# Starting the second DMA queue of an ifftshift copy three steps further on

## The chip, the cores and the metric

The kernel runs on one core of a Trainium2 chip. The metric is the device time of one execution in microseconds, lower is better. A difference between two kernels is judged from the medians of their runs.

## The reference

The kernel computes an inverse FFT shift of a square float32 matrix. For an even size this exchanges the quadrants: the upper half of the rows changes place with the lower half, and the left half of the columns with the right half.

```python
x = np.random.randn(8192, 8192).astype(np.float32)
out = np.fft.ifftshift(x)      # out[r, c] = x[(r + 4096) % 8192, (c + 4096) % 8192]
```

Nothing is calculated. Each of the 8192 rows is 32 KiB long and is copied in two halves of 16 KiB, 268.44 MB in all, and the same amount is read and written.

## The kernel before, in words

The copy goes from HBM to HBM by DMA. No tile in on-chip memory is used, and no compute engine takes part, apart from four small memsets that the framework puts at the start.

The rows of the output are taken in steps of 16 (`ENGINES`, line 9), one row for each of the core's 16 DMA engines. One DMA covers 32 steps (`per`, line 25), so 512 rows, and one half of the columns. Its access pattern (line 26) has three dimensions: 16 rows next to each other, then 32 steps of 16 rows, then 4096 elements in a piece. The first dimension is the one that is spread over the DMA engines. Each engine thus gets 32 packets of 16 KiB from one DMA, for rows that are 16 apart, and a last small packet that updates the semaphore of that DMA.

The loop over `row` (line 27) makes 16 rounds. In each round two DMAs are issued (lines 29 and 30): the left half of the output (`h = 0`) on the SP queue, and the right half (`h = hc`) on the scalar queue. In the profile the SP queue is q1 and the scalar queue q10 (its issues are shown under ACTq). The left half of an output row is read from the right half of the source row, and the other way round. The source row is half the matrix away: `src_row = (row + hr) % R`, 4096 rows or 128 MiB.

Both queues feed the same 16 DMA engines. No DMA depends on the data of another. The framework gives every DMA one of eight semaphores in turn, four to each queue, so an issue waits until the DMA four places before it on the same queue has landed. The order of the packets on an engine is set by the order of the DMAs on each queue and by how the engine takes turns between the two queues.

Of the kernel before, what the change touches and what calls it, by code (L numbers as in the profile page):

```python
# [1 line left out]

# [4 lines left out]


ENGINES = 16


@with_exitstack
def kernel(
    ctx: ExitStack,
    tc: tile.TileContext,
    x: bass.AP,
    out: bass.AP,
):
    nc = tc.nc
    R, C = x.shape  # L20
    hr = R // 2
    hc = C // 2


    per = 32
    dims = [[C, ENGINES], [ENGINES * C, per], [1, hc]]
    for row in range(0, R, ENGINES * per):
        src_row = (row + hr) % R
        for queue, h in ((nc.sync, 0), (nc.scalar, hc)):
            queue.dma_start(  # L30
                out=bass.AP(out.tensor, out.offset + row * C + h, dims),
                in_=bass.AP(x.tensor, x.offset + src_row * C + hc - h, dims),
            )


# [1 line left out]
_INS = ['x']  # L37
_OUTS = [((8192, 8192), 'float32')]


def kernel(**inputs):
    import numpy as _np
    import concourse.bacc as _bacc
    import concourse.tile as _tile
    from concourse import mybir as _mybir
    from concourse.bass_utils import run_bass_kernel_spmd as _run

    nc = _bacc.Bacc("TRN2", target_bir_lowering=False, num_devices=1)  # L48
    arrays, args = {}, []
    for name in _INS:  # L50
        a = _np.ascontiguousarray(inputs[name])
        if a.dtype.kind in "iu":
            a = a.astype(_np.int64)
        arrays[f"in_{name}_dram"] = a
        args.append(nc.dram_tensor(f"in_{name}_dram", a.shape, _mybir.dt.from_np(a.dtype), kind="ExternalInput").ap())
    for i, (shape, dtype) in enumerate(_OUTS):
        dt = _mybir.dt.from_np(_np.dtype(dtype))
        args.append(nc.dram_tensor(f"out_{i}_dram", shape, dt, kind="ExternalOutput").ap())
    with _tile.TileContext(nc) as tc:
        kernel(tc, *args)  # L60
    r = _run(nc, [arrays], core_ids=[0])
    got = tuple(r.results[0][f"out_{i}_dram"] for i in range(len(_OUTS)))
    return got[0]
```

## Time and profile before

| what | value |
|---|---|
| median of 3 runs | 821.4 us (821.02 to 823.58) |
| the profiled execution | 822.98 us, its span 821.2 us |
| DMA packets | 16896, 268.44 MB, mean 327 GB/s |
| HBM read and written together | 654 GB/s over the span |
| share of the 16 engines' span, SP queue (q1) | 50.2% |
| share of the 16 engines' span, scalar queue (q10) | 49.0% |
| DMA issues | 16 on each queue, 8192 KB each, about 204 us from issue to landing |

The span runs from the first to the last instruction of the program. The share of a queue is the time that its packets took, as a part of 16 engines' span; both shares together say how full the DMA engines are. The two rows of forty figures in the prediction cut the span into 40 equal slices, 20.5 us each: the first row is the busy share of the DMA engines in tenths (9 is 90% or more), the second is what they moved in GB/s. A DMA view can also be asked for a short stretch of the span. It then gives, for each queue, the number of packets that start in it, the MB they moved and the share. A line of issues gives the number of instructions and the KB of each. A line of the timeline gives start and duration in microseconds. An issue's duration includes the time in which it waits for room in the queue.

### The profile page before, as it was taken

The numbers are of one execution on the slowest core, as the hardware profiler recorded it, in microseconds if no ns is written. First come the engines' busy times: TensorE is split into PE (matmuls) and PEld (weight loads), VectorE is DVE, ScalarE is ACT, GpSimd is POOL, SyncE is SP. The second block draws the span as 40 slices with busy tenths as digits, with TensorE's granted clock in tenths as the row PEclk, the third lists the DMA queues.
The fourth block names the chain that finished last, engine by engine and source line by source line (L and its number), as shares of the span: only waits on it lengthen the run. The fifth ranks groups of instructions, "written<-read, shape, count | busy, mean of one in ns | idle before, by whom it ended". The sixth has DMA issues, their size and how long they took to land. (4 is left out here: it accounts for less than half of the span.)

```text
span 821.2 us, 77 instructions
## 1 busy us (share of the span) xinstructions
POOL 0.2 (0%) x4
## 2 busy tenths in 40 slices
POOL 0000000000000000000000000000000000000000
DMA  8999999999999999999999999999999999999998
GB/s 296 333 324 329 331 328 334 330 330 329 327 330 329 331 326 332 332 327 328 330 330 330 330 323 330 324 330 330 332 326 329 330 322 333 329 329 327 330 329 276
DMA packets 16896, 268.44 MB, mean 327 GB/s; under 512 B 512, under 2 KB 512, under 8 KB 512
## 3 DMA queue, kind: packets, MB, share of 16 engines
q1 hardware_dynamic: 8448, 134.22, 50.2%
q10 hardware_dynamic: 8448, 134.22, 49.0%
HBM read 268.44 MB, written 268.44 MB: 654 GB/s over the span
## 5 line engine op out<-in xcount | busy, mean ns | idle before, releaser
L48 POOL MEMSET const-bfloat16-1.0<- 128x1 bf16 x1 | 0.1, 102 | 0.0
L48 POOL MEMSET const-uint8-127<- 128x1 uint8 x1 | 0.1, 102 | 0.0
L48 POOL MEMSET const-float32-0.0<- 128x1 f32 x1 | 0.1, 99 | 0.2 <-issue 0.2
L48 POOL MEMSET const-float32-1.0<- 128x1 f32 x1 | 0.1, 99 | 0.0
## 6 DMA issues: line engine op xcount, KB each, us to landing
out_dram<-in_x_dram ACTq DMA_DIRECT2D x16, 8192.0 KB, 204.1
out_dram<-in_x_dram SPq DMA_DIRECT2D x16, 8192.0 KB, 204.0
```

The source lines that it names most:

```text
L48: nc = _bacc.Bacc("TRN2", target_bir_lowering=False, num_devices=1)
```

## The change

A step is still 16 rows. The left halves are issued as before: 16 DMAs of 32 steps on the SP queue. The right halves, on the scalar queue, begin with step 3 (`lead = 3`) and come round to steps 0 to 2 at the end. The function `pieces` cuts the steps so that no DMA crosses a multiple of 32 steps, where the source row would wrap at the middle of the matrix. The scalar queue thus has 17 DMAs: one of 29 steps, fifteen of 32 and one of 3. The issues of the two queues still alternate in the program, and bytes, packet sizes and the split over the engines stay as they are.

```diff
     per = 32
-    dims = [[C, ENGINES], [ENGINES * C, per], [1, hc]]
-    for row in range(0, R, ENGINES * per):
+    lead = 3
+    steps = R // ENGINES
+
+    def copy(queue, h, first, n):
+
+        dims = [[C, ENGINES], [ENGINES * C, n], [1, hc]]
+        row = first * ENGINES
         src_row = (row + hr) % R
-        for queue, h in ((nc.sync, 0), (nc.scalar, hc)):
-            queue.dma_start(
-                out=bass.AP(out.tensor, out.offset + row * C + h, dims),
-                in_=bass.AP(x.tensor, x.offset + src_row * C + hc - h, dims),
-            )
+        queue.dma_start(
+            out=bass.AP(out.tensor, out.offset + row * C + h, dims),
+            in_=bass.AP(x.tensor, x.offset + src_row * C + hc - h, dims),
+        )
+
+    def pieces(first, last):
+
+        while first < last:
+            n = min(per, last - first, per - first % per)
+            yield first, n
+            first += n
+
+    lefts = list(pieces(0, steps))
+    rights = list(pieces(lead, steps)) + list(pieces(0, lead))
+    for k in range(max(len(lefts), len(rights))):
+        if k < len(lefts):
+            copy(nc.sync, 0, *lefts[k])
+        if k < len(rights):
+            copy(nc.scalar, hc, *rights[k])
```

## The prediction

> **What bounds the kernel now.** I read the page from the top. No compute engine matters: the only busy one is POOL, with four memsets at the start. What counts are the DMA lines.
>
> ```profile
> span 821.2 us, 77 instructions
> POOL 0.2 (0%) x4
> DMA  8999999999999999999999999999999999999998
> GB/s 296 333 324 329 331 328 334 330 330 329 327 330 329 331 326 332 332 327 328 330 330 330 330 323 330 324 330 330 332 326 329 330 322 333 329 329 327 330 329 276
> DMA packets 16896, 268.44 MB, mean 327 GB/s; under 512 B 512, under 2 KB 512, under 8 KB 512
> q1 hardware_dynamic: 8448, 134.22, 50.2%
> q10 hardware_dynamic: 8448, 134.22, 49.0%
> HBM read 268.44 MB, written 268.44 MB: 654 GB/s over the span
> out_dram<-in_x_dram ACTq DMA_DIRECT2D x16, 8192.0 KB, 204.1
> out_dram<-in_x_dram SPq DMA_DIRECT2D x16, 8192.0 KB, 204.0
> ```
>
> The reader is to see that the 16 DMA engines are busy from the third microsecond to the last few, at an even 322 to 334 GB/s between the two end slices. The time is therefore the number of packets on one engine times the mean time of a packet, and a change can help only through that mean, the head or the tail. Of the 8448 packets of a queue, 256 are semaphore updates (16 DMAs on 16 engines) and 8192 move 16 KB. From the shares, a data packet took 0.502 x 16 x 821.2 / 8192 = 805 ns on q1 (SP) and 0.490 x 16 x 821.2 / 8192 = 786 ns on q10 (scalar). An engine moves 512 of each: 412.2 + 402.4 = 814.6 us. The first packet starts at 2.1 us, so the engines end near 816.7 on average; some 4.5 us of the 821.2 are then the spread of the engines and the closing. The profiled execution took 822.98 us, 1.8 more than its span and 1.6 above the median of 821.4.
>
> The second thing to read is how the queues stand to each other. I asked the DMA view for the stretch from 2 to 4.9 us and for one from 815.1 to 818 us:
>
> ```profile
> q1 hardware_dynamic: 60, 0.98, 98.1%
> ...
> q10 hardware_dynamic: 59, 0.82, 81.1%
> q1 hardware_dynamic: 19, 0.08, 8.2%
> ```
>
> In the first stretch only q1 runs: 60 packets, nearly four per engine, before q10 sends anything. At the end it is turned round: q10 moves 0.82 MB while q1 has 0.08 MB left. The issues late in the run show the same distance, since each waits for the landing of the DMA four places before it on its queue:
>
> ```profile
> 614.16 39.30 SPq L30 DMA_DIRECT2D out_dram<-in_x_dram  x1
> 618.85 39.97 ACTq L30 DMA_DIRECT2D out_dram<-in_x_dram  x1
> ```
>
> That is 4.69 us, and a pair of packets takes 805 + 786 = 1591 ns, so the distance is 2.95, that is three steps. I also followed single engines through the packet records (the next packet starts 3 to 4 ns before the recorded end of the one before). Nearly every engine starts q1, q1, q1, q1, q10, and then alternates; between q1's semaphore update and q10's lie three data packets of each queue, all through the run. So an engine now copies the left half of step k+3, then the right half of step k, then the left of k+4, and so on: the two places are 48 rows of 32 KiB, 1.5 MiB, apart.
>
> **The change part by part.**
>
> *Order of the rights.* The scalar queue starts at step 3 and ends with steps 0 to 2. With q1 still four packets ahead at the start, an engine copies left 3, right 3, left 4, right 4: one whole row, half after half. Packets and bytes stay the same: 1024 data packets of 16 KB per engine. What can move is the mean of a packet, and no row of this trace has the two halves together. Bounds from both sides, from rows:
>
> - Gain. The fewest places at once that the trace shows is one queue alone. At the start (3.2 to 4.9 us) 44 packets of q1 took 1.033 x 16 x 1.7 / 44 = 639 ns; this is the first moment after idle. At the end (815.1 to 818 us) q10 moved 0.82 MB, 50 data packets, in 0.811 x 16 x 2.9 = 37.6 us: 752 ns. Against the mean of 795.5 in the whole run the latter is 43 ns less; for 1024 packets that is 44 us, and 160 us by the former.
> - Loss. The slowest stretch of several microseconds that I saw in the middle, 400 to 404 us, ran at 315 GB/s against 328 in 400 to 500 us. A whole run like that would be 4.1% longer, 34 us.
>
> ```profile
> q1 hardware_dynamic: 44, 0.72, 103.3%
> ...
> q1 hardware_dynamic: 1036, 16.45, 50.9%
> q10 hardware_dynamic: 1030, 16.35, 48.7%
> ```
>
> (3.2 to 4.9 us, then 400 to 500 us.) Between these ends I take the one difference the trace shows between packets that run in the same mix: q10's packets are 805 - 786 = 19 ns shorter than q1's. I assume that the second packet of a row, following its other half, gains as much again. This is a choice of size, not a measurement. It is nearer to the middle of the run than the head and tail rows, which are short and lie where engines start or fall idle. 512 x 19 ns = 9.7 us off.
>
> Why a gain at all: four address streams (left read, left write, right read, right write) in two stretches of rows for x and two for out become one stretch of x and one of out. Within a pair, the two writes of an engine cover one row of 32 KiB. If the memory pays for every new place it opens, there are fewer. That it pays for this is not shown here.
>
> *Seventeen DMAs instead of sixteen on the scalar queue* (29, fifteen times 32, and 3 steps). Each engine gets one semaphore packet more: 9 ns in the packet records, and the data packet behind one averages 26 ns above the mean of all, together 35 ns once. The extra issue is hidden: an issue that finds room takes 0.58 us (the shortest in the trace), and the one that waits does so with three DMAs of about 50 us each queued before it. It waits for its queue's thirteenth DMA, and is issued near 669 us, where its data is due at about 811 us. If that cover were gone, it would cost the issue and the time to the first packet: 0.58 + (2.1 - 0.73) = 1.9 us. Nothing on the scalar engine or SP stands behind it but the end of the kernel.
>
> *Both queues' ends of a DMA at one time.* Now q1 gives up a turn to a semaphore packet three steps before q10 does; afterwards both do so in the same round, 16 times. The trace shows no gap round such a packet, so I take 0; with 26 ns for each it is 0.4 us.
>
> *Head and tail.* SP still starts first and the scalar queue still ends with three packets per engine alone; 0 for both.
>
> A rule that speaks against the change: the Trainium skill's "DMA: Bandwidth & Descriptors", section "Latency and other measured facts", says that copies between HBM tensors fall from 214 to 103 GB/s per direction when streams in lock step are a large power of two apart (4 MiB row pitch), with channel aliasing as an unverified reason. After the change an engine's read of one half and its write of the same half, a packet apart, lie 4096 rows, 128 MiB, apart within their tensors; by that rule at full strength an estimate would be 821 x 214 / 103 = 1,707 us. Source and destination rows are 4096 apart now too, and the page shows 327 GB/s, so I keep it only as the reason of the slower rival, not as its price.
>
> *Sum.* 822.98 - 9.7 = 813.3 for the profiled execution, and 1.6 less for the median: 811.7, so 812 us.
>
> **The rivals.**
>
> 1. *The halves together help* (forecast): 812 us; its own range runs from 797 to 818.9, the lower end being half of the 44 us plus a little.
> 2. *The memory is at a fixed rate and does not care.* For it: the even rate in 38 of 40 slices, while the lefts and rights cross every position in the array, and the 1.5 MiB distance was held throughout, so nothing shows that distance matters. Time: 821.4 plus 0.4, within 0.3% (about what a measurement can tell from no change), 818.9 to 823.9.
> 3. *The change does not do what it says*: the shorter first DMA makes the scalar queue start at another distance, say two steps. Against it: the distance was set before the first DMA had ended, by the order in which the queues began, and this is not touched. A distance of one row step or so would be priced like case 2.
> 4. *Slower: the halves collide.* Now, when an engine reads the lower half of a row of x, it has just been writing the lower half of a row of out three steps on; afterwards it has just written the lower half of the corresponding row. If rows 4096 apart fall on the same parts of the memory, the read and the draining write meet there, once per pair. Price: if q10's packets lose the 19 ns by which they are shorter, 512 x 19 = 9.7 us, hence 831; at the bound 855. It decides once the mean of the packet rises by 2.4 ns (2.5 us over 1024). For it: in the packet records a third of the data packets take the shortest time, 611 ns, and one in twenty of q1 over 1.2 us, so waiting for something shared is common. Against it: each packet's own read and write are already such a pair.
>
> **How the numbers follow.** Case 1: 0.44, case 2: 0.14, case 3: 0.04, case 4: 0.38. Two signs are nearly even, because the size and the sign of the one effect are not in this trace; I lean to the gain, since fewer places at once is the one direction that the head and tail rows point to (639 and 752 ns against 795). Faster 0.44, same 0.18, slower 0.38. Eight times in ten: from 796 (half of the tail's gain and a little) to 838 (half of the loss bound), leaving about one in ten on each side. The predicted time is that of case 1.
>
> **What the profile after would show.** Right: 17 issues on the scalar queue, the first landing about 3 steps (4.8 us) earlier than now, close to SP's; later landings of both queues at nearly the same time; the same 134.22 MB per queue and one DMA more in semaphore packets (8464 on q10); q10's packets nearer 767 ns than 786, and GB/s slices near 332. Wrong: slices at 327 to 330 mean case 2; slices at 322 to 325 with q10 at 805 ns or q1 longer still mean case 4; landings of the two queues one or more steps apart mean case 3. The forecast fails if the place of the two queues in the memory does not enter the packet's time, or enters it with the other sign.

## The result

The changed kernel took 827.39 us (median of 11 runs, 826.74 to 832.63), the kernel before 822.08 us (median of 11, 819.85 to 826.24). The ratio is 1.0073, with a 95% interval of 1.0055 to 1.0092: slower by 0.7%. Here and below, a ratio and its interval are worked out from all runs of both kernels but those over 1.5% above the fastest of their own kernel, so a ratio need not equal the quotient of the two medians beside it (1.0065 here). The forecast of 812 us had the wrong sign. The range holds the time, and rival 4 (slower, 831 us) is the case that is nearest.

The page of the changed kernel. A line of the issues gives the count, the KB of each and the microseconds from issue to landing.

```profile
span 829.4 us, 78 instructions
DMA  9999999999999999999999999999999999999998
GB/s 290 329 313 318 322 315 317 326 323 335 324 320 321 328 328 326 315 333 326 330 330 317 330 333 324 329 322 335 326 333 326 330 325 332 330 332 327 330 323 273
DMA packets 16912, 268.44 MB, mean 324 GB/s; under 512 B 528, under 2 KB 528, under 8 KB 528
q10 hardware_dynamic: 8464, 134.22, 50.3%
q1 hardware_dynamic: 8448, 134.22, 48.9%
HBM read 268.44 MB, written 268.44 MB: 647 GB/s over the span
out_dram<-in_x_dram SPq DMA_DIRECT2D x16, 8192.0 KB, 205.1
out_dram<-in_x_dram ACTq DMA_DIRECT2D x15, 8192.0 KB, 205.2
out_dram<-in_x_dram ACTq DMA_DIRECT2D x1, 7424.0 KB, 54.0
out_dram<-in_x_dram ACTq DMA_DIRECT2D x1, 768.0 KB, 155.3
```

The engines are as full as before. By the same working as in the prediction, a packet of q1 now takes 0.489 x 16 x 829.4 / 8192 = 792 ns, 13 less than before, and one of q10 0.503 x 16 x 829.4 / 8192 = 815 ns, 29 more. The pair is 16 ns longer, and 512 x 16 = 8.2 us is the difference of the two spans (829.4 - 821.2). The shares are rounded; added up from the packet records, the data packets of an engine take 821.9 us instead of 814.2, 7.7 of the 8.2 us. So nearly all of the time came from the mean of a packet. (This profiled execution took 831.17 us, 3.8 above the median of its kernel.)

The order on the engines is what the change meant. The timeline late in the run shows an issue of SP and two of the scalar queue in one line (x2), start and duration. Each issue waits for the DMA four places before on its queue, and the first ones now begin 0.17 us apart, where it was 4.69 us.

```profile
622.47 38.91 SPq L34 DMA_DIRECT2D out_dram<-in_x_dram  x1
622.64 93.18 ACTq L34 DMA_DIRECT2D out_dram<-in_x_dram  x2
```

Where in the run the time went is seen when the span is cut into stretches. The columns are start and end, length, POOL's busy time, clock, DMA share and GB/s. Some stretches are left out. First the changed kernel, then the kernel before:

```profile
10.00:60.00 50.00, 0.00 (x0) 1.00 1.00 315
100.00:200.00 100.00, 0.00 (x0) 1.00 1.00 322
200.00:300.00 100.00, 0.00 (x0) 1.00 1.00 325
300.00:400.00 100.00, 0.00 (x0) 1.00 1.00 325
400.00:500.00 100.00, 0.00 (x0) 1.00 1.00 328
600.00:700.00 100.00, 0.00 (x0) 1.00 1.00 329
700.00:800.00 100.00, 0.00 (x0) 1.00 1.00 330
```

```profile
10.00:60.00 50.00, 0.00 (x0) 1.00 1.00 326
100.00:200.00 100.00, 0.00 (x0) 1.00 1.00 330
300.00:400.00 100.00, 0.00 (x0) 1.00 1.00 330
700.00:800.00 100.00, 0.00 (x0) 1.00 1.00 328
```

The changed kernel starts 3% slower and is level after about 400 us, though its order of rows is the same to the end. From the packet records, in stretches of about one DMA (51 us, the first one from 10 us on, counted from the first packet), with q1's and q10's mean packet added; the last column is the standard deviation over the 16 engines of the moment at which they reach the end of that DMA on q1:

| stretch | before, ns per pair | changed, ns per pair | before, spread us | changed, spread us |
|---|---|---|---|---|
| 1 | 1606 | 1654 | 0.40 | 0.47 |
| 2 | 1585 | 1637 | 0.49 | 0.78 |
| 4 | 1590 | 1612 | 0.74 | 0.91 |
| 8 | 1591 | 1599 | 0.79 | 0.86 |
| 12 | 1587 | 1581 | 0.79 | 0.87 |
| 16 | 1589 | 1590 | 0.77 | 1.08 |

The engines start together and drift apart, and the excess fades too. But the spread alone does not set the excess: at the end of the second stretch the changed kernel's 0.78 us is as wide as what the kernel before settles at, and in the third stretch a pair still takes 1636 ns, against 1576 before.

### The profile page after: what moved, and what is told of

The parts are those of the page before. It is cut to its first block, busy times and chain, and to the rows that moved or that the text cites. A ratio compares the mean times of both kernels' runs of the same rounds, so it can differ in the third digit from the quotient of the medians.

```text
span 829.4 us, 78 instructions
## 1 busy us (share of the span) xinstructions
POOL 0.2 (0%) x4
## 6 DMA issues: line engine op xcount, KB each, us to landing
out_dram<-in_x_dram ACTq DMA_DIRECT2D x1, 768.0 KB, 155.3
```

## The experiments

Four theories were set against each other. A: the scalar queue's read of a half of x meets the draining write of the same half of out (rival 4 of the prediction). B: the two reads in one row of x disturb each other. C: the two writes into one row of out do. D: the addresses don't matter, but both queues now end a DMA in the same round. In all runs of the first group the DMAs of both queues are cut at the same rounds, and the two offsets of the scalar queue, for reading and for writing, can be set apart (shortened, with comments added; the lines with a minus are those of the changed kernel):

```diff
-    lead = 3
+    ahead = 3          # SP's place minus the scalar queue's, in steps, at one time
+    read_lead = 3
+    write_lead = 3
-    rights = list(pieces(lead, steps)) + list(pieces(0, lead))
+    cuts = {p - ahead for p in range(per, steps, per)} | wraps   # where a source or target wraps
+    # rights: cut at cuts; lefts: cut at cuts + ahead
-            copy(nc.scalar, hc, *rights[k])
+            p, end = rights[k]
+            copy(nc.scalar, hc, (p + read_lead) % steps, (p + write_lead) % steps, end - p)
```

**Control (both 3).** The DMAs are exactly those of the changed kernel.

> Control: the changed kernel again (the scalar queue reads and writes three steps on, so both halves of a row of x and of out follow each other). All theories: about 827 us, ratio to before 1.006 to 1.009. The new profile has to show whether the excess sits in the early part of the run, as in the first profile of the changed kernel, where the two queues' packets took 1654 ns per pair in the first DMA and 1590 ns in the last (before: 1591 ns throughout); if that was a disturbance of one execution, the pairs will be equally long from start to end.

Measured: 828.63 us against 823.03, ratio 1.0043 (1.0013 to 1.0073). The new profile has the same course: 1659 ns per pair in the first stretch, 1600 in the last. The excess at the beginning belongs to the kernel and not to one execution. Three of the twelve executions took 820 to 824 us, the others 826 to 831; a possible reason stands in the last section.

**The ends of the DMAs alone.**

```diff
-    read_lead = 3
-    write_lead = 3
+    read_lead = 0
+    write_lead = 0
```

> The addresses of before (the queues 48 rows apart), but the DMAs cut so that both queues end a DMA in the same round, as in the changed kernel. If the coinciding ends cost (theory D): about 827 us, ratio 1.007. If addresses alone cost (theories A, B, C): 822 us, ratio 1.000 within 0.002.

Measured: 823.03 us against 823.03, ratio 1.0008 (0.9989 to 1.0027), and 1589 ns per pair in the first stretch. Theory D falls.

**Reads in the same rows, writes 48 rows apart.**

```diff
-    write_lead = 3
+    write_lead = 0
```

> The scalar queue reads three steps on, at the rows that SP reads, but writes where it wrote before, 48 rows behind SP; the right half of the output is thus rolled by 48 rows. Theory A (the read of a half of x meets the draining write of the same half of out): about 827 us, ratio 1.007, since the scalar queue reads the half that SP has just written. Theory B (the two reads in one row of x get in each other's way): 827 us too. Theory C (the two writes in one row of out do): 822 us. Theory D (ends of DMAs): 827 us.

Measured: 820.87 us against 823.03, ratio 0.9974 (0.9953 to 0.9995). Not slower but, if anything, a little faster: the interval ends just below 1. B falls, and A as it was put (the scalar queue reading the half that SP has just written) with it. The stretches of this run:

```profile
10.00:60.00 50.00, 0.00 (x0) 1.00 1.00 329
100.00:200.00 100.00, 0.00 (x0) 1.00 1.00 329
700.00:800.00 100.00, 0.00 (x0) 1.00 1.00 330
```

**Writes in the same rows, reads 48 rows apart.**

```diff
-    read_lead = 3
+    read_lead = 0
```

> The reverse: the scalar queue reads 48 rows behind SP, as before, but writes at the rows that SP writes; the right half of the output is rolled by 48 rows. Theory C (the two writes): about 827 us, ratio 1.007. Theories A and B (both through the read of the scalar queue): 822 us, ratio 1.000 within 0.002. Theory D: 827 us.

Measured: 850.41 us (847.35 without its two slowest runs of six) against 823.03, ratio 1.0301 (1.0264 to 1.0339). C has the sign, but the size is four times what it expected. The rate, from the fastest of the six executions, shows a loss that is deeper than in the changed kernel (313 against 322 GB/s from 100 to 200 us) and above all longer; it comes near the level of before only after 600 us:

```profile
10.00:60.00 50.00, 0.00 (x0) 1.00 1.00 311
100.00:200.00 100.00, 0.00 (x0) 1.00 0.99 313
400.00:500.00 100.00, 0.00 (x0) 1.00 1.00 320
600.00:700.00 100.00, 0.00 (x0) 1.00 0.99 327
700.00:800.00 100.00, 0.00 (x0) 1.00 1.00 327
```

In the packet records the engines also stay together for longer here: the spread is 0.42 us at the end of the fifth DMA, where the changed kernel has 0.76. But at step 288 of 512, at 477 us, it is 0.78 us, as wide as in the kernel before, and a pair from 450 to 550 us still takes 1646 ns, against 1593 there. So a small spread cannot be the whole condition of the loss.

**The same with the reads ahead.** In the run before, the scalar queue's own source and target were 4096 - 48 rows apart, which could have been the cause of the size.

```diff
-    read_lead = 3
+    read_lead = 6
```

> The scalar queue writes at SP's rows, as in the changed kernel, but reads 48 rows ahead of SP's reads instead of 48 behind (the right half of the output is rolled by 48 rows). It takes the size of the earlier run with reads 48 behind (1.030) apart. Theory C (writes into one row, one after the other, while the engines are close together; unequal reads leave them close for longer): about as slow as that run, 840 to 850 us, ratio 1.02 to 1.03. If that run was slow because its reads lay 4096 - 48 rows from its writes: 827 us or less, since here they lie 4096 + 48 apart, as in the run with only the reads aligned (0.997).

Measured: 844.82 us (843.62 without its slowest run of six) against 821.99, ratio 1.0263 (1.0230 to 1.0297). The sign of the read distance hardly matters; writes in the same rows with unequal reads are the slow form. One thing can't be taken apart here: with the writes together, reads that are apart also mean that the scalar queue's own source and target are not exactly 4096 rows apart. The run with only the reads aligned shows that such a distance (4096 + 48) costs nothing when the writes are apart.

**No exchange of the columns.** A second form of the cross theory was left: the scalar queue writes the half of a row of out whose counterpart in x SP has just read. This edit takes it away.

```diff
-            in_=bass.AP(x.tensor, x.offset + src_row * C + hc - h, dims),
+            in_=bass.AP(x.tensor, x.offset + src_row * C + h, dims),
```

> The changed order without the exchange of the column halves: left from left, right from right (the output's column halves are thus exchanged). Each packet still shares its rows with the other queue's, but the scalar queue no longer writes the half of a row whose counterpart in x SP has just read. Theory C (two writes into one row of out, one after the other): about 827 us, ratio above 1.004. Cross theory (the write of a half meets the read of the same half by the other queue): 822 us, ratio 1.000 within 0.002.

Measured: 829.16 us against 821.95, ratio 1.0083 (1.0057 to 1.0108), with 1647 ns per pair in the first stretch. The cross theory does not account for the loss in this form either, and the course is that of the changed kernel (1637 ns there and 1636 here in the second stretch, 1588 and 1594 in the tenth). A run without the exchange and with the queues 48 rows apart was not made, so what the missing exchange itself may cost is not taken off. What all slow runs share is that both queues write into the same rows at the same time.

**Restarts.** If the excess needs engines that are close together, it must come back when they are lined up again. Both kernels were cut into four quarters with a wait for all DMAs between them.

```diff
-    with _tile.TileContext(nc) as tc:
-        tile_ifftshift_kernel(tc, *args)
+    for quarter in range(4):
+        with _tile.TileContext(nc) as tc:
+            tile_ifftshift_kernel(tc, *args, quarter)
     # in the kernel: steps quarter * 128 to quarter * 128 + 127, rights with lead 0 or 3
```

> The kernel before, cut into four quarters of 128 steps with a wait for all DMAs between them, so that the 16 engines start together four times. All theories: 822 plus three closings and heads of about 6 us, 840 us; packets 1591 ns per pair in every quarter.

> The changed kernel in the same four quarters, the scalar queue three steps on within each. Lockstep theory (the excess is there while the 16 engines are close together, and goes as they drift apart): it comes back in every quarter; the first four DMAs of the changed kernel had 63 + 46 + 44 + 21 ns per pair above 1591, times 32 steps 5.6 us, so 4 x 5.6 = 22 us over the quartered kernel before. Rival (the excess belongs to the rows at the beginning or to the time since launch): only the first half has it, 5 to 9 us over the quartered kernel before.

Measured: 832.38 us with lead 0 and 851.52 us with lead 3, ratios to before 1.0124 (1.0097 to 1.0151) and 1.0347 (1.0311 to 1.0382). The three restarts cost 10 us with lead 0, not 18. The lead costs 19.1 us, against 22 and 5 to 9. The pages' rows of GB/s, lead 0 and then lead 3 (slices of 21 us; the dips in slices 10, 20 and 30 or next to them are the restarts):

```profile
GB/s 301 334 328 326 328 327 323 333 333 297 311 330 328 330 327 331 329 322 331 294 319 330 323 332 332 326 319 318 336 296 307 331 329 327 329 329 330 334 322 293
```

```profile
GB/s 298 324 307 313 317 323 324 318 321 314 285 322 318 326 316 320 325 327 330 289 315 320 313 317 312 329 326 329 319 278 309 316 315 322 313 326 322 320 329 285
```

In the packet records the first 32 steps of the four quarters take 1620, 1623, 1627 and 1660 ns per pair with lead 3, and 1583, 1589, 1577 and 1590 with lead 0. Over the four quarters, the first 64 steps average 1641 ns per pair with lead 3 and the last 64 1608, with lead 0 1589 and 1590: the excess is back in each quarter and falls within it. Added up, the data packets of an engine take 831.7 us with lead 3 and 813.8 with lead 0, 17.9 of the 18.9 us between the two profiled spans (849.7 and 830.8). So the excess depends on the time since a common start, and not on the rows or on the time since launch. That it is the spread of the engines, and not something else that a restart sets back, was not shown, and the spread at step 288 of the run with only the writes aligned speaks against it as the whole cause.

**Other distances.** With the two offsets equal, the scalar queue can stand at any distance.

```diff
-    read_lead = 3
-    write_lead = 3
+    read_lead = 2      # further runs: 4, 7, 259
+    write_lead = 2
```

> The scalar queue two steps on instead of three, with DMA ends kept in the same round: the queues are one step, 16 rows or 512 KiB, apart. If the two halves must be of one row for the excess (theory C, strict): 822 us, ratio 1.000 within 0.002. If nearness of the writes in general costs: 824 to 827 us. If the engines' order in a step matters rather than the row: as the changed kernel, 827 us.

> The scalar queue four steps on: one step, 16 rows, ahead of SP, in executions where it starts three steps late. If nearness of the writes costs while the engines are close: 823 to 826 us, with 1600 to 1640 ns per pair in the first two DMAs. If only halves of one row do: 822 us and 1591 ns throughout.

> The scalar queue seven steps on, four steps (64 rows, 2 MiB) ahead of SP. Theory C: far enough, as before: 822 us, ratio 1.000 within 0.002. If a power of two between the queues costs: above 827 us.

> The scalar queue half the matrix (256 steps, 128 MiB) ahead of SP. Theory C: 822 us, ratio 1.000 within 0.002. If large powers of two between streams cost: above 827 us. If far apart is better than 48 rows: below 819 us, and then it beats both kernels.

| offset | us | before, us | ratio | 95% interval |
|---|---|---|---|---|
| 2 | 824.49 | 821.95 | 1.0019 | 0.9994 to 1.0043 |
| 4 | 821.47 | 821.99 | 0.9990 | 0.9973 to 1.0006 |
| 7 | 822.16 | 821.99 | 0.9995 | 0.9976 to 1.0013 |
| 259 | 821.66 | 821.99 | 0.9991 | 0.9975 to 1.0008 |

Neither 2 MiB (offset 7) nor 128 MiB (offset 259) between the queues costs or brings anything that can be measured, and no distance beats the kernel before. The runs with 2 and 4 did not answer whether one step apart costs, because in their profiled executions the queues did not start three steps apart. The DMA view from 2 to 4.9 us, with offset 4:

```profile
q10 hardware_dynamic: 60, 0.98, 100.0%
```

and with offset 2:

```profile
q1 hardware_dynamic: 43, 0.70, 81.8%
q10 hardware_dynamic: 16, 0.26, 22.9%
```

With offset 4 the scalar queue had gone first and was three packets ahead, which puts it seven steps ahead in rows; with offset 2 it came only one packet behind SP, which puts it one step ahead. That last one is the only look at a distance of one step: 1643 and 1639 ns per pair in the first two stretches, then 1593. It speaks for nearness counting beyond the row itself, but one execution is no measurement of it.

## Why the prediction was wrong

**What held.** The reading of the bottleneck held: only the mean of a packet could move the time. The mean of a packet accounts for 7.7 of the 8.2 us between the profiled executions. What held too: the three steps, the new order on the engines (landings of both queues together; the scalar queue's first comes 54.0 us after issue instead of 56.5, so 2.5 us earlier where 4.8 were foreseen, as the pairs before it had become longer), and the parts put at nothing: the seventeenth DMA, hidden with 155.3 us from issue to landing, and the coinciding ends, which the run with the ends alone puts at a ratio of 1.0008.

**The step that failed** is the one under *Order of the rights*: "I assume that the second packet of a row, following its other half, gains as much again." The second packet did not gain 19 ns but lost 29, and the first gained 13. The sum had this term at minus 9.7 us; it came to plus 8.2 us between the profiled executions, and to plus 5.3 us between the medians. Two things were wrong in it.

First, the price was taken from a row that is no price. The 19 ns between q10 and q1 are a share of the engines' time that can turn round while the pair stays as long; they are not what an address costs. With offset 7, where the time is that of before, q1 takes 773 ns and q10 811; in the run with the ends alone they take 803 and 783. The pairs are 1584 and 1586 ns. The split turned round and the sum stayed. Why it turns was not looked into.

Second, the ground for the sign was "fewer places at once", with the reads and the writes taken together. They go opposite ways. Reads in the same rows are harmless or a little better (0.9974); writes in the same rows cost 2.6 to 3.0% when the reads are apart, and 0.4 to 0.8% when the reads are together as well. The head and tail rows (639 and 752 ns) showed one queue alone, thus half the writes at a time, and could say nothing on two writes in one row.

**Rival 4** had the sign and 831 us, but its mechanism, a read against a draining write, was not the cause: the run with only the reads aligned kept it and was not slower, and the run without the exchange took that meeting of the two queues away and was slower all the same. That 831 us lies near the measured time is luck, since this price was made from the same 19 ns. **Rival 2** would have been right for the two distances with a clear reading, offsets 7 and 259. Its argument, that nothing in the trace showed that distance matters, rested on a trace that held one distance throughout. **Rival 3** was unlikely for the wrong reason: the order in which the queues begin is not fixed, as the profiles with offsets 2 and 4 show.

The rule that was weighed from the Trainium skill's "DMA: Bandwidth & Descriptors", section "Latency and other measured facts", is about a row pitch of large powers of two. No run here tests that pitch: the 16 rows of a step lay 32 KiB apart in all of them. What the runs show is that 2 MiB and 128 MiB between the two queues cost nothing (0.9995 and 0.9991).

**What stays open:** why two writes into the same rows cost; why they cost most in the first hundreds of microseconds after a common start; why unequal reads, or the distance within the scalar queue that comes with them, make that loss larger and longer; whether writes one step apart cost as well; and where the 0.26% comes from that reads in the same rows gave, if it is real. That gain can't be had in an ifftshift, since reads and writes move together.

## What to carry to other kernels

Where DMA engines are full at an even rate, judge a change of order by reads and writes apart: bringing two queues' writes into the same rows cost time here, bringing their reads there did not. A difference between two queues' packet times was a split here and not a cost; look at the sum over a round. And an order that relies on two queues starting a fixed distance apart relies on something that two of the fourteen profiles here didn't keep.

## What was not expected of the hardware

- Loss that fades within a run: 315 GB/s from 10 to 60 us and 330 from 700 to 800 us in the same kernel at the same order, and back to 1620 to 1660 ns per pair after each restart. A mean over a whole run hides it. A shorter copy in this order may lose a larger share; no shorter copy was run, but the quartered kernel lost 19.1 us where the whole one lost 5.3.
- The start order of the two queues varies. SP was four packets ahead in most profiles, two in one, and in one the scalar queue led by four. If the three executions of the control at 820 to 824 us were of that kind, their rows were not aligned; no profile was taken of them, so this is a guess.
- A semaphore update takes a queue's turn on the engine. In the packet records of the kernel before, q1's update (9 ns) stands between two packets of q10, so that q10 moves one packet nearer until its own update, three packets of each queue later. Two queues whose DMAs end in different rounds are one step nearer between those ends.
